# Modulation of a three-block model in unsplit float32 on four column groups, and HGRN states kept in place

## The chip, the cores and the metric

One core of a Trainium2 chip. The metric is the device time of one execution in microseconds (us). Kernel lines (L286) are those of the kernel before.

## The reference, cut to what matters

Two hybrid layers over 1024 latent and 256 context positions, width 1024, then a second block (state space model, latent attention, feed forward). All is float32. Each layer is modulated by vectors computed from a condition:

```
shift, scale, gate = split(c_act @ w_mod + b_mod, 3)          # latent: one row, 1024 x 3072, per layer
shift_c, scale_c, gate_c = split(cc_act @ w_mod + b_mod, 3)   # context: another row, same weights
lat = split_cols((rms_norm(h, norm_g) * (1 + scale) + shift) @ w_in)
...
s_new = exp(a_last) * state + einsum("bhsk,bhsv->bhkv", kc * exp(a_last - a), vc)   # HGRN, chunk by chunk
inter = einsum("bhtk,bhkv->bhtv", qc * exp(a), state)
...
h_new = h + gate * y
```

The second block has one more such modulation (1024 x 6144). Three products of two rows by a wide matrix are 24 row blocks of 512 columns.

## The kernel before, in words

Activations lie transposed, channels on partitions. Precision: a float32 operand is split into a high part (`wh`, cast on ACT to float32r) and a low part (`wl`, the remainder, subtracted on POOL or DVE), and a product is three matmuls of parts. `weights` (L194) makes them: 512 columns at a time it loads a raw tile (`wr`), casts `wh` (L203) and subtracts `wl` (L204). The pool `wp` holds 3 raw, 6 high and 6 low tiles, shared by all projections (`project`, L331: two tiles each, matmuls on L344, block by block) and by the modulation.

`modulation` (L275) makes one row block per step of a generator. For each of 4 pieces of 1024 columns it takes the split weights and multiplies both parts by the stationary condition (128 x 4: both rows, high and low): 16 matmuls (L286) into rows 0 to 3 of a PSUM tile. ACT copies the row (L288), four transposes (L291) turn it, and DVE adds bias and parts (L294, L296):

```
row = self.psum()[0:4]
parts = self.weights(w[j // 4, c], 1024, 512, subs, raws)
PE.matmul(row, act[:, 2 * c + k, :], parts[k][i], ...)
PE.transpose(t[:, 4 * i:4 * i + 4], r[:, i * P:(i + 1) * P], self.ident[0:4, 0:4])
```

The first four blocks run at the start (`inputs` in `first_block`, L1014), with a pool of 14 raw tiles and subtractions on DVE and POOL in turn. The other 20 are `self.filler`: `fill` (L173) takes one after every second projection of the two layers; their subtractions are on DVE.

The order of work: `hybrid_mix` (L972) runs a main chain, Fourier, attention (`gqa`), HGRN (`hgrn`), and beside it a lane of projections. At places of the main chain `dense(us)` takes as much of the lane as the budget says, by the numbers that the lane yields (a modulation block yields 24 x 0.213). The tile framework then schedules all instructions in that priority onto each engine's queue, with the buffers that each tag has, and writes the waits. Loads and stores are on SP's queue.

HGRN (L679) works on two channel halves c. Per direction it forms gates, sums them in chunks of 128 by a scan on DVE (L718), makes turned keys (tag `sc`), chunk sums `u` (L742), and then the states entering each chunk, `st` (L751), one step per chunk, of `st`, `ea` and `u`; a block's output (L833) takes them. The mask of its levels (L816) is uint32.

Of the kernel before, what the change touches and what calls it, by code (L numbers as in the profile page):

```python
# [14 lines left out]
U32 = mybir.dt.uint32  # L15
# [6 lines left out]
P = 128  # L22
# [58 lines left out]
GQA_STEPS = 4, 4, 0.5  # L81
MLA_STEPS = 3, 5, 0.4
# [7 lines left out]
class Kern:  # L90


    def __init__(self, tc, ctx):
        self.tc = tc
        self.nc = nc = tc.nc
        self.V, self.G, self.S, self.PE = nc.vector, nc.gpsimd, nc.scalar, nc.tensor
        self.const = ctx.enter_context(tc.tile_pool(name="const", bufs=1))
        self.tp = ctx.enter_context(tc.tile_pool(name="tp", bufs=2))
        self.dram = ctx.enter_context(tc.tile_pool(name="dr", bufs=1, space=DRAM))
        self.ps = ctx.enter_context(tc.tile_pool(name="ps", bufs=2, space=PSUM))  # L100
        self.flip = 0
        self.pending = None
        self.filler = iter(())
        self.calls = 0
        self.lane, self.owed = iter(()), 0.0
# [5 lines left out]
    def setup(self, io):  # L111
        V, G, S = self.V, self.G, self.S

        def const(name, shape, dt=F32):
            t = self.const.tile(list(shape), dt, name=name)
            self.load(t, io[name])
            return t

        self.vecs = const("vecs", (P, NVEC))
        self.ident = const("ident", (P, P))  # L120
        self.bd2 = const("bd2", (P, 2))
        self.one = self.const.tile([P, 1], F32, name="one")
# [3 lines left out]
        self.act = []  # L126
        for b in range(2):
            t = self.const.tile([P, 8, 4], F32R, name=f"act{b}")
            for s in range(2):
                a = act[:, 2 * b + s, :].rearrange("p (k o) -> p k o", o=1)  # L130
                S.activation(t[:, :, s:s + 1], a, AF.Copy)
                V.tensor_tensor(t[:, :, 2 + s:3 + s], a, f32(t)[:, :, s:s + 1], op=ALU.subtract)
            self.act.append(t)
# [60 lines left out]
    def weights(self, ap, n, width=P, subs=None, raws=None):  # L194

        out = []
        for a in range(0, n, WTILE):
            m = min(WTILE, n - a)
            raw = (raws or self.wp).tile([P, WTILE], F32, tag="wr", name="wr", bufs=14 if raws else 3)[:, :m]
            hi = self.wp.tile([P, WTILE], F32R, tag="wh", name="wh", bufs=6)[:, :m]  # L200
            lo = self.wp.tile([P, WTILE], F32R, tag="wl", name="wl", bufs=6)[:, :m]
            self.load(raw, ap[:, a:a + m])
            self.S.activation(hi, raw, AF.Copy)  # L203
            (next(subs) if subs else self.G).tensor_tensor(lo, raw, f32(hi), op=ALU.subtract)  # L204
            out += [(hi[:, k:k + width], lo[:, k:k + width]) for k in range(0, m, width)]
        return out
# [68 lines left out]
    def modulation(self, w, act, bias, tiles, out, subs=None, raws=None):  # L275


        V, PE = self.V, self.PE
        subs = subs or cycle((V,))
        for j in tiles:  # L280
# [6 lines left out]
            r = self.tmp("sp")[0:4]  # L287
            self.S.activation(r, row, AF.Copy)  # L288
# [3 lines left out]
            tv = t[:, :16].rearrange("p (i a) -> p i a", a=4)  # L292
            u = self.tmp("mu", (P, 4, 2))
            V.tensor_tensor(u, tv[:, :, 0:2],  # L294
                            bias[:, j:j + 4].rearrange("p (i o) -> p i o", o=1).to_broadcast([P, 4, 2]), op=ALU.add)
            V.tensor_tensor(out[:, j:j + 4], u, tv[:, :, 2:4], op=ALU.add)  # L296
            yield 24 * MM
# [170 lines left out]
    def weigh(self, pool, out, keys, n, scores, v, beside, pieces, steps):  # L468
# [5 lines left out]
        tail, ahead, wait = steps  # L474
# [6 lines left out]
        def count(i, e):  # L481
# [3 lines left out]
            elif len(sums[E]) == 1:  # L485
                total = self.ctmp(pool, "ea" if E is G else "eb", (P, 512), 2)[:, :n]
# [6 lines left out]
        for i, j in enumerate(keys):  # L493
            s = scores(j)
            e = self.ctmp(pool, "e", (P, 512), 13)[:, :n]
# [183 lines left out]
    def hgrn(self, pool, layer, src, need_ctx, y):  # L679
# [18 lines left out]
        mask = pool.tile([P, len(HG_LEVELS), P], U32, name="hg_mask")  # L698
        self.load(mask, self.io["hg_mask"])
        rst = pool.tile([P, 512], F32, name="rst")  # L700
        G.memset(rst, 1.0)
        G.memset(chunked(rst)[:, :, 0:1], 0.0)
        for c in range(2):
# [10 lines left out]
            for d, nm in ((0, "ff"), (1, "fb")):  # L714
                a, k = self.hgrn_gates(pool, src[f"{nm}{c}"], layer, d, c)
                for t0, n in ALL:
                    s = a[:, t0:t0 + n] if d == 0 else a[:, t0:t0 + n][:, ::-1]
                    V.tensor_tensor_scan(s, rst[:, :n], s, 0.0, op0=ALU.mult, op1=ALU.add)  # L718
# [12 lines left out]
                for t0, n in ALL:  # L731
                    kts.append(self.ctmp(pool, "sc", (P, 512), 3))
                    turned(kts[-1][:, :n], e, t0, n)
                for (t0, n), kt in zip(ALL, kts):
# [8 lines left out]
            state = []  # L743
            for d in range(2):
                st = pool.tile([P, nc_, 64], F32, tag=f"st{d}", name="st")
# [3 lines left out]
                G.memset(st[:, order[0]], 0.0)  # L749
# [3 lines left out]
                state.append(st)  # L753
# [5 lines left out]
    def hgrn_block(self, pool, layer, c, t0, n, src, vt, state, mask, cum, key, y):  # L759
# [10 lines left out]
        acc = [self.ctmp(pool, "sc", (P, 512), 3)[:, :n] for _ in range(2)]  # L770
# [56 lines left out]
        for j in range(m):  # L827
            cs = slice(j * P, (j + 1) * P)
            for h in range(2):
                r = slice(64 * h, 64 * h + 64)  # L830
                PE.matmul(o[r, cs], vt[:, j * P + 64 * h:j * P + 64 * h + 64], acc[h][:, cs], start=True, stop=False)
                for d in range(2):
                    PE.matmul(o[r, cs], state[d][r, c0 + j], qd[d][r, cs], start=False, stop=d == 1)  # L833
# [15 lines left out]
    def fourier(self, pool, src, t0, n, chan, alt, pos, y):  # L849
# [39 lines left out]
        for c in range(2):  # L889
# [24 lines left out]
            w = pool.tile([P, T], F32, tag="fy", name="fy", bufs=2)  # L914
            sn = pool.tile([P, T // 2], F32, tag="fs", name="fs", bufs=2)
# [8 lines left out]
    def hybrid_out(self, pool, layer, y, src, w_out, h_old, gate, t0, n, beside):  # L924
# [5 lines left out]
        for k in HYBRID_ORDER:  # L930
# [6 lines left out]
            a = pool.tile([P, 512], F32R, tag="yb", name="yh", bufs=20)[:, :n]  # L937
            b = pool.tile([P, 512], F32R, tag="yb", name="yl", bufs=20)[:, :n]
# [33 lines left out]
    def hybrid_mix(self, layer, io, x, need_ctx, inputs, close_x):  # L972
# [15 lines left out]
        with pool_of("fo") as fp:  # L988
# [4 lines left out]
            a = self.ctmp(fp, "fs", (P, T // 2), 2)  # L993
# [3 lines left out]
            a = self.ctmp(fp, "fs", (P, T // 2), 2)  # L997
# [16 lines left out]
    def first_block(self, io):  # L1014
# [12 lines left out]
        def inputs():  # L1027
            with tc.tile_pool(name="start", bufs=6, side="left", reuse_waits="tile") as sp:
                first = self.modulation(io["w_mod"][0], self.act[0], self.vec("b_mod", 0, 24), (8, 12, 0, 4), mod[0],
                                        cycle((V, self.G, V)), sp)  # L1030
# [26 lines left out]
            self.modulation(io["w_mod"][0], self.act[0], self.vec("b_mod", 0, 24), (16, 20), mod[0]),  # L1057
            self.modulation(io["w_mod"][1], self.act[0], self.vec("b_mod", 24, 24), range(0, 24, 4), mod[1]),
            self.modulation(io["w_mod_2"], self.act[1], self.vec("b_mod_2"), range(0, 48, 4), mod2))
# [20 lines left out]
        y, src = self.hybrid_mix(1, io, x, False, inputs1(y, src, xp, x), xctx.close)  # L1080
        self.rp = self.rows.enter_context(tc.tile_pool(name="rows", bufs=1, side="right", reuse_waits="tile"))
# [728 lines left out]
    def weight_pool(self, bufs):  # L1810
        ctx = ExitStack()
        self.wp = ctx.enter_context(self.tc.tile_pool(name="wp", bufs=bufs, side="left", reuse_waits="tile"))
        return ctx
# [79 lines left out]
    def run(self, io, out):  # L1893
        self.io = io
        self.setup(io)
        with ExitStack() as self.rows, self.weight_pool(3):
            self.second_block(io, *self.first_block(io), out)

# [22 lines left out]
def _constants():  # L1921
# [7 lines left out]
    m = np.zeros((P, len(HG_LEVELS), P), np.uint32)  # L1929
# [3 lines left out]
    c["hg_mask"] = m  # L1933
    k = np.arange(512)
# [118 lines left out]
```

## Time and profile before

| | |
|---|---|
| median of 3 runs | 4120.85 us (4118.63 to 4126.01) |
| profiled execution | 4121.71 us, span 4119.5 us |
| TensorE (PE) busy | 3827.2 us, 93% |
| weight loads (PEld) | 2892.6 us, 70% |
| DVE, ACT, POOL | 2426.4, 1683.2, 1536.1 us |
| mean granted clock of TensorE | 0.962 of full speed |
| HBM | 377.39 MB read, 119.21 MB written |

Busy times of matmuls are sums of single durations, which overlap in the pipeline; how long a run of matmuls takes is read from their starts. A float32 matmul is recorded as two instructions. Each group's idle time is that of its engine just before its instructions, with what ended it. The granted clock has two levels, 1.2 and 2.4 GHz; a mean of 0.95 over a stretch says that a tenth of it was at the lower one.

### The profile page before, as it was taken

How to read it: one execution, taken by the hardware profiler on the slowest of the kernel's cores; microseconds unless marked ns; L12 is line 12 of the kernel's file. 1: busy time of each engine (PE TensorE's matmuls, PEld its weight loads, DVE VectorE, ACT ScalarE, POOL GpSimd, SP SyncE). 2: the span in 40 equal slices, each digit the busy share in tenths (PEclk: the TensorE clock that was granted, in tenths of full speed). 3: DMA queues.
4: the chain of work that ended last, by engine and by line, in shares of the span. 5: the costliest groups of instructions: out<-in, count | busy, mean ns of one | idle time of the engine just before them, and what ended most of it. 6: DMA issues, size and time to landing. Idle time of an engine off the chain costs nothing.

```text
span 4119.5 us, 55376 instructions
## 1 busy us (share of the span) xinstructions
PE 3827.2 (93%) x19562; PEld 2892.6 (70%) x19562; DVE 2426.4 (59%) x4210; ACT 1683.2 (41%) x3047; POOL 1536.1 (37%) x1336
## 2 busy tenths in 40 slices
PE   6999999999999988988899988999999989999998
PEld 3765576667775567767667666665567979988986
DVE  7355587855446587768867776665565374324321
ACT  5333444345424445345434253444444343333332
POOL 3223301125314422146222133555555444445443
PEclk8999999999999989989999999999999989999999
DMA  5541222256552221164354567452223463343232
GB/s 180 170 130 61 65 75 93 83 165 212 174 161 64 70 74 58 63 206 146 118 161 147 183 184 209 116 147 63 50 51 110 136 208 102 93 117 121 93 114 83
DMA packets 273913, 500.25 MB, mean 121 GB/s; under 512 B 30978, under 2 KB 76578, under 8 KB 270628
## 3 DMA queue, kind: packets, MB, share of 16 engines
q1 hardware_dynamic: 269636, 467.75, 36.2%
q0 software_dynamic: 4000, 28.97, 3.0%
q8 instruction: 154, 2.52, 0.3%
q14 instruction: 123, 1.01, 0.1%
HBM read 377.39 MB, written 119.21 MB: 121 GB/s over the span
## 4 chain that ended last, share of the span: by engine, by line
PE 37%; DVE 11%; DMA 4%; ACT 2%; issue 2%; POOL 1%; SPq 0%; DVEq 0%; ACTq 0%; POOLq 0%
PE mm L213 22%; PE mm L344 5%; PE o L510 4%; DVE sm L459 3%; DVE sp L1161 2%; PE mm L1346 1%; DVE eb L487 1%; PE o L1563 1%; PE t L1585 1%; PE t L1357 1%; PE t L1358 1%; PE t L1520 1%; PE t L1356 1%; ACT sw L1553 1%; DMA xt<-xtok 0%
## 5 line engine op out<-in xcount | busy, mean ns | idle before, releaser
L204 POOL TENSOR_TENSOR wl<-wr,wh 128x512 fp32r<-128x512 f32 (+2 forms) x641 | 860.3, 1349 | 1568.0 <-ACT wh L203 1299.5
L203 ACT ACTIVATE wh<-wr 128x512 fp32r<-128x512 f32 (+1 forms) x822 | 503.2, 620 | 812.6 <-PE mm L213 250.7
L344 PE MATMUL mm<-xh,wh 128*128 128x512 f32 (+1 forms) x1704 | 664.1, 391 | 10.0 <-DVE sp L169 2.9
L344 PE MATMUL mm<-xh,wl 128*128 128x512 f32 (+1 forms) x1704 | 648.3, 381 | 6.6 <-POOL wl L204 6.5
L344 PE MATMUL mm<-xl,wh 128*128 128x512 f32 (+1 forms) x1704 | 648.9, 381 | 1.0 <-POOL xl L324 0.9
L496 ACT ACTIVATE e<-t 128x512 f32<-128x512 f32 (+1 forms) x488 | 284.0, 594 | 278.6 <-PE t L1358 125.7
L344 PEld LDWEIGHTS mm<-xh,wh 128*128 128x128 f32 x1704 | 329.9, 194 | 93.0 <-issue 19.7
L490 POOL TENSOR_TENSOR ea<-ea,e 128x512 f32<-128x512 f32 x240 | 325.5, 1356 | 170.1 <-ACT e L496 161.8
L344 PEld LDWEIGHTS mm<-xh,wl 128*128 128x128 f32 x1704 | 329.3, 193 | 75.0 <-POOL wl L204 10.6
L344 PEld LDWEIGHTS mm<-xl,wh 128*128 128x128 f32 x1704 | 330.2, 194 | 71.1 <-issue 13.5
L213 PE MATMUL mm<-fxh,wh 128*128 128x512 f32 (+2 forms) x1056 | 339.2, 322 | 2.9 <-ACT fxh L1737 2.1
L213 PE MATMUL mm<-fxh,wl 128*128 128x512 f32 (+2 forms) x1056 | 341.0, 323 | 0.0
L213 PE MATMUL mm<-fxl,wh 128*128 128x512 f32 (+2 forms) x1056 | 340.4, 322 | 0.3 <-DVE fxl L1738 0.2
L459 DVE TENSOR_REDUCE sm<-mm 128x1 f32<-128x512 f32 (+1 forms) x384 | 207.6, 589 | 17.3 <-PE mm L1346 16.7
L213 PEld LDWEIGHTS mm<-fxh,wh 128*128 128x128 f32 x1056 | 201.2, 191 | 19.2 <-ACT fxh L1737 2.6
L213 PEld LDWEIGHTS mm<-fxl,wh 128*128 128x128 f32 x1056 | 201.5, 191 | 17.4 <-DVE fxl L1738 1.6
L213 PEld LDWEIGHTS mm<-fxh,wl 128*128 128x128 f32 x1056 | 201.7, 191 | 15.6
L204 DVE TENSOR_TENSOR wl<-wr,wh 128x512 fp32r<-128x512 f32 x181 | 137.3, 771 | 68.8 <-ACT wh L203 66.1
L510 PE MATMUL o<-e,v 128*64 128x512 f32 x640 | 175.8, 602 | 0.0
L487 POOL TENSOR_TENSOR ea<-e 128x512 f32<-128x512 f32 (+1 forms) x52 | 65.8, 1265 | 237.0 <-ACT e L496 204.5
L1775 DVE TENSOR_SCALAR fc<-gs,vecs 128x512 f32<-128x512 f32 x44 | 54.1, 1231 | 165.8 <-ACT gs L1771 165.8
L459 DVE TENSOR_REDUCE sm<-t 128x1 f32<-128x512 f32 (+1 forms) x200 | 112.3, 589 | 55.3 <-PE t L596 53.8
(470 smaller groups left out, 8079.7 us busy)
## 6 DMA issues: line engine op xcount, KB each, us to landing
wr<-w_mod SPq DMA_DIRECT2D x192, 256.0 KB, 3.0
wr<-w_in SPq DMA_DIRECT2D x190, 256.0 KB, 2.9
wr<-w_up SPq DMA_DIRECT2D x176, 256.0 KB, 2.7
wr<-w_out SPq DMA_DIRECT2D x144, 256.0 KB, 3.1
wr<-w_down SPq DMA_DIRECT2D x80, 256.0 KB, 2.7
q<-qd POOLq DMA_DIRECT2D x16, 768.0 KB, 6.4
rope<-rope SPq DMA_DIRECT2D x20, 512.0 KB, 4.2
k<-kd POOLq DMA_DIRECT2D x16, 640.0 KB, 7.4
```

Of the source, the lines that this page charges most:

```text
L203: self.S.activation(hi, raw, AF.Copy)
L204: (next(subs) if subs else self.G).tensor_tensor(lo, raw, f32(hi), op=ALU.subtract)
L213: self.PE.matmul(out, a, b, start=i == 0, stop=i == n - 1)
L344: self.PE.matmul(ps, a, b, start=at + i == 0, stop=at == k_tiles - 1 and i == 2)
L459: V.tensor_reduce(m[:, a, c:c + 1], scores(a, c), axis=AX.X, op=ALU.max, negate=True)
L487: E.tensor_tensor(total, sums[E][0], e, op=ALU.add)
L490: E.tensor_tensor(sums[E][0], sums[E][0], e, op=ALU.add)
L496: S.activation(e, s, AF.Exp)
L510: PE.matmul(o[h:h + 64], v(j), e, start=i < 2, stop=i >= len(keys) - 2)
L1161: V.scalar_tensor_tensor(c, u[:, s0 + a:s0 + a + n], cw[:, a:a + 1], c, op0=ALU.mult, op1=ALU.add)
L1346: PE.matmul(s, qt[h][:, 0, t0 + a * P:t0 + (a + 1) * P], kt[h][:, 0, c0:c0 + w])
L1775: V.tensor_scalar(c, gs[:, o:o + 512], w[:, 0:1], b, op0=ALU.mult, op1=ALU.add)
```

## The change

1. Modulation. The weights are not split: a float32 tile of 512 columns (`mr`) is the moving operand. The stationary operand (`mact`) is 128 x 32 per piece, the two rows and 30 zero columns; piece k of 8 goes to column group k % 4 (rows 32(k % 4) onward of the PSUM tile), so each group gets two accumulating matmuls. ACT copies all 128 rows (`mrow`), and four matmuls with a constant 128 x 2 (`mod_sum`: ones at rows 0, 32, 64, 96 and 1, 33, ...) turn and sum them; this is done one block later. DVE adds the bias. The loads of a block are issued at the projection after the block before (`prefetch`); at the start 14 pieces are ahead. A block yields 16 x 0.213, and each of the three calls has one more step.
2. `wp` gets 4 high and 4 low tiles in the two layers, 6 and 6 in the second block (closed and opened again between, after the filler has run out), besides 8 `mr` tiles.
3. HGRN: states are written over the chunk sums `u`, the zero state is left out (8 clears, 8 matmuls less); the scan runs in pieces of 256; `sc` has 2 buffers instead of 3, the keys are turned one block ahead; the mask is uint8.
4. Buffers: attention's exponentials 13 to 10 in GQA, one `eb`; Fourier's `fy` and `fs` 2 to 1; output's split inputs 20 to 18.

```diff
-    def modulation(self, w, act, bias, tiles, out, subs=None, raws=None):
+    def modulation(self, w, block, bias, tiles, out, more=None):
...
-            row = self.psum()[0:4]
-            for c in range(4):
-                parts = self.weights(w[j // 4, c], 1024, 512, subs, raws)
-                for k in range(2):
-                    for i in range(2):
-                        PE.matmul(row, act[:, 2 * c + k, :], parts[k][i], start=c + k + i == 0, stop=c + k + i == 5)
...
-                PE.transpose(t[:, 4 * i:4 * i + 4], r[:, i * P:(i + 1) * P], self.ident[0:4, 0:4])
...
+        act = self.mod_act(block)
+        pieces = [(j, k) for j in tiles for k in range(8)]
+        ahead = 14 if more else 8
...
+        def turn(j, r):
+            t = self.psum()
+            for i in range(4):
+                PE.matmul(t[:, 2 * i:2 * i + 2], r[:, i * P:(i + 1) * P], self.mod_sum)
...
+        due.extend(range(ahead))
+        load()
+        self.prefetch = load
+        behind = None
+        for i, (j, k) in enumerate(pieces):
+            if k == 0:
+                load()
+                row = self.psum()
+            c = slice(32 * (k % 4), 32 * (k % 4) + 32)
+            PE.matmul(row[c], act[:, k], ws.pop(i), start=k < 4, stop=k >= 4)
+            due.append(i + ahead)
+            if more:
+                load()
+            if k == 7:
+                if behind:
+                    turn(*behind)
+                r = self.ctmp(self.wp, "mrow", (P, 512), 1)
+                self.S.activation(r, row, AF.Copy)
+                behind = j, r
+                yield 16 * MM
+        turn(*behind)
+        yield 1.0
...
         wks = [self.weights(w, k_tiles * P) for w in ws]
+        self.prefetch()
...
-            hi = self.wp.tile([P, WTILE], F32R, tag="wh", name="wh", bufs=6)[:, :m]
+            hi = self.wp.tile([P, WTILE], F32R, tag="wh", name="wh", bufs=self.wbufs)[:, :m]
...
-                for t0, n in ALL:
-                    s = a[:, t0:t0 + n] if d == 0 else a[:, t0:t0 + n][:, ::-1]
+                for t0 in range(0, TA, 256):
+                    s = a[:, t0:t0 + 256] if d == 0 else a[:, t0:t0 + 256][:, ::-1]
...
-                for a, b in zip(order, order[1:]):
-                    V.scalar_tensor_tensor(st[:, b], st[:, a], ea[:, d, a:a + 1], u[:, d, a],
-                                           op0=ALU.mult, op1=ALU.add)
+                for i, (a, b) in enumerate(zip(order, order[1:])):
+                    if i:
+                        V.scalar_tensor_tensor(u[:, d, a], state[d][a], ea[:, d, a:a + 1], u[:, d, a],
+                                               op0=ALU.mult, op1=ALU.add)
+                    state[d][b] = u[:, d, a]
```

Two places show how instructions move. DVE's order at the first HGRN gates of layer 0 (`wl` is a low part, `a0` the gates, the scan is the one on `rst`), before:

```order
L204 TENSOR_TENSOR wl_4333<-wr_4331,wh_4332 128x512
L666 SCALAR_TENSOR_TENSOR a0_4235<-gx_4233,gx_4234 128x1280
L204 TENSOR_TENSOR wl_4339<-wr_4337,wh_4338 128x512
L667 TENSOR_TENSOR k0_4236<-a0_4235,gx_4233 128x1280
L204 TENSOR_TENSOR wl_4349<-wr_4347,wh_4348 128x512
L718 SCALAR_TENSOR_TENSOR a0_4235<-rst_4193,a0_4235 128x512 x2
L718 SCALAR_TENSOR_TENSOR a0_4235<-rst_4193,a0_4235 128x256
L204 TENSOR_TENSOR wl_4355<-wr_4353,wh_4354 128x512
L722 TENSOR_TENSOR gx_4248<-a0_4235 128x1280
L294 TENSOR_TENSOR mu_4370<-mm_4365,vecs_66 128x8
```

and now:

```order
L697 SCALAR_TENSOR_TENSOR a0_3901<-gx_3899,gx_3900 128x1280
L698 TENSOR_TENSOR k0_3902<-a0_3901,gx_3899 128x1280
L749 SCALAR_TENSOR_TENSOR a0_3901<-rst_3849,a0_3901 128x256 x5
L753 TENSOR_TENSOR gx_3916<-a0_3901 128x1280
L163 COPY cux_4096<-mm_4165 128x256
L756 TENSOR_TENSOR gx_3916<-gx_3916,k0_3902 128x1280
L303 TENSOR_TENSOR mod1_88<-mm_4214,vecs_66 128x8
```

The low parts of a modulation block stood between the gates' steps, one behind the scan; now none does, and of the modulation DVE keeps the bias. SP's queue at the start (`h` are the tiles of x), before:

```order
L142 DMA bd_70<-bd 128x2
L142 DMA wr<-w_mod 128x512 x24
L142 DMA h_0_337<-xT 128x512
...
L142 DMA h_7_351<-xT 128x512
L142 DMA wr<-w_mod 128x512 x8
L142 DMA wr<-w_in 128x512 x3
```

and now:

```order
L136 DMA bd_70<-bd 128x2
L136 DMA mod_sum<-mod_sum 128x2
L136 DMA mr<-w_mod 128x512 x32
L136 DMA h_0_217<-xT 128x512
...
L136 DMA h_7_231<-xT 128x512
L136 DMA wr<-w_in 128x512 x3
```

The last eight pieces of the first four blocks stood behind x and stand ahead of it now.

## Rows read from the trace of the kernel before

**Rows 1.** The page, part 1: busy us, share of the span, instructions.
```profile
PE 3827.2 (93%) x19562; PEld 2892.6 (70%) x19562; DVE 2426.4 (59%) x4210; ACT 1683.2 (41%) x3047; POOL 1536.1 (37%) x1336
```
**Rows 2.** Stretches: us; busy us of PE, PEld, DVE, ACT, POOL; PEclk; DMA.
```profile
60.00:500.00 440.00, 410.89 (x1863) 273.79 (x1861) 224.87 (x427) 169.27 (x297) 136.78 (x131) 0.94 0.32 102
500.00:910.00 410.00, 378.47 (x2305) 283.50 (x2306) 315.71 (x698) 172.06 (x291) 52.73 (x43) 0.96 0.31 100
...
1060.00:1460.00 400.00, 377.26 (x1674) 247.43 (x1673) 208.96 (x360) 165.23 (x269) 131.27 (x113) 0.95 0.37 116
1460.00:1760.00 300.00, 270.04 (x1555) 209.15 (x1554) 221.85 (x437) 125.03 (x178) 57.20 (x47) 0.96 0.21 67
```
**Rows 3.** Groups by line, PE, 60 to 1500 us: busy us, mean ns, idle before.
```profile
L344 PE MATMUL mm<-xh,wl 128*128 128x512 f32 (+1 forms) x977 | 363.6, 373 | 1.8 <-POOL wl L204 1.7
...
L286 PE MATMUL mm<-wl,act 128*4 128x512 f32 x160 | 66.8, 418 | 28.8 <-DVE wl L204 28.6
L286 PE MATMUL mm<-wh,act 128*4 128x512 f32 x160 | 65.8, 411 | 8.8 <-ACT wh L203 8.7
...
L291 PE MATMUL mm<-ident,sp 4*128 4x4 f32 x80 | 9.5, 221 | 7.2 <-ACT sp L288 7.1
```
**Rows 4.** Timeline, PE, one modulation block in HGRN: start, us, instruction, idle before.
```profile
503.77 0.40 PE L286 MATMUL mm<-wl,act 128*4 128x512 f32 x1 [1.22 <-DVE wl L204]
504.00 0.39 PE L286 MATMUL mm<-wh,act 128*4 128x512 f32 x1
...
510.20 0.59 PE L286 MATMUL mm<-wl,act 128*4 128x512 f32 x1 [3.42 <-DVE wl L204]
```
**Rows 5.** Timeline, DVE, the same block.
```profile
503.03 0.69 DVE L204 TENSOR_TENSOR wl<-wr,wh 128x512 fp32r<-128x512 f32 x1
...
505.63 3.93 DVE L718 TENSOR_TENSOR_SCAN a<-rst,a 128x512 f32<-128x512 f32 x3
```
**Rows 6.** Timeline, PE, attention of the second block: float32 matmuls in two column groups.
```profile
2559.43 1.93 PE L510 MATMUL o<-e,v 128*64 128x512 f32 x6
2561.29 0.38 PE L1346 MATMUL mm<-k,q 128*128 128x256 f32 x1
2561.61 1.08 PE L510 MATMUL o<-e,v 128*64 128x512 f32 x4
2562.61 0.51 PE L1346 MATMUL mm<-k,q 128*128 128x512 f32 x1
```
**Rows 7.** Timeline, PE: the transposes of a first block; small float32 matmuls.
```profile
14.83 0.41 PE L291 MATMUL mm<-ident,sp 4*128 4x4 f32 x4 [0.68 <-ACT sp L288]
15.17 0.40 PE L286 MATMUL mm<-wh,act 128*4 128x512 f32 x1
...
181.70 1.84 PE L249 MATMUL t<-bd,sq 128*128 128x2 f32 x16
```
**Rows 8.** 13 half-clock stretches, columns as in rows 2: last, sum; L286 alone.
```profile
1446.50:1460.20 13.70, 7.51 (x25) 3.78 (x26) 11.78 (x15) 7.99 (x13) 2.54 (x2) 0.50 0.44 139
sum 95.60, PE 76.45 PEld 52.16 DVE 64.42 ACT 43.05 POOL 39.57; mean PE 5.88 PEld 4.01 DVE 4.96 ACT 3.31 POOL 3.04
...
sum 95.60, PE 15.09 PEld 2.13; mean PE 1.16 PEld 0.16
```
**Rows 9.** Timeline, PE, the start: sums of squares and first projections.
```profile
35.42 1.86 PE L249 MATMUL t<-one,acc 128*128 128x1 f32 x8 [5.04 <-DVE acc L314]
...
48.34 0.50 PE L344 MATMUL mm<-xh,wh 128*128 128x512 f32 x1
...
87.28 0.61 PE L249 MATMUL t<-one,acc 128*128 128x1 f32 x4
...
91.43 1.22 PE L344 MATMUL mm<-xh,wh 128*128 128x256 f32 x3 [1.18 <-ACT xh L326]
```
**Rows 10.** Groups by line, ACT and POOL, 60 to 1500 us.
```profile
L203 ACT ACTIVATE wh<-wr 128x512 fp32r<-128x512 f32 x296 | 182.2, 626 | 244.8 <-PE mm L344 105.9 <-DMA wr<-w_mod 42.6 <-DMA wr<-w_in 35.8
...
L204 POOL TENSOR_TENSOR wl<-wr,wh 128x512 fp32r<-128x512 f32 x136 | 193.6, 1436 | 586.6 <-ACT wh L203 417.6 <-DVE sc L814 54.8 <-DVE hw L795 40.5
```

More of the change, by code (lines that the diff above doesn't have):

```diff
@@ L1 @@
 from contextlib import ExitStack
-from itertools import chain, cycle
+from itertools import chain
 import numpy as np
@@ L125, in setup @@
         S.activation(act.rearrange("p a k -> p (a k)"), self.vec("act"), AF.Silu)
[L126 to L133, printed above, removed]
+        self.act = act
+        self.mod_sum = const("mod_sum", (P, 2))
         self.qg = self.const.tile([P, 2], F32, name="qg")
@@ L192, in dense_to, with weights @@
             self.owed = 0.0
-    def weights(self, ap, n, width=P, subs=None, raws=None):
+    def weights(self, ap, n, width=P):
         out = []
@@ L271, in split, with mod_act @@
         self.V.tensor_tensor(lo, x, f32(hi), op=ALU.subtract)
-    def modulation(self, w, act, bias, tiles, out, subs=None, raws=None):
-        V, PE = self.V, self.PE
-        subs = subs or cycle((V,))
-        for j in tiles:
-            row = self.psum()[0:4]
-            for c in range(4):
-                parts = self.weights(w[j // 4, c], 1024, 512, subs, raws)
-                for k in range(2):
-                    for i in range(2):
-                        PE.matmul(row, act[:, 2 * c + k, :], parts[k][i], start=c + k + i == 0, stop=c + k + i == 5)
-            r = self.tmp("sp")[0:4]
-            self.S.activation(r, row, AF.Copy)
+    def mod_act(self, block):
+        t = self.ctmp(self.wp, "mact", (P, 8, 32), 1)
+        self.G.memset(t, 0.0)
+        for s in range(2):
+            self.V.tensor_copy(t[:, :, s:s + 1], self.act[:, 2 * block + s, :].rearrange("p (k o) -> p k o", o=1))
+        return t
@@ new lines, in modulation, with load @@
+    def modulation(self, w, block, bias, tiles, out, more=None):
+        V, PE = self.V, self.PE
+        act = self.mod_act(block)
+        pieces = [(j, k) for j in tiles for k in range(8)]
+        ahead = 14 if more else 8
+        ws, due = {}, []
+        def load():
+            for i in due:
+                if i < len(pieces):
+                    j, k = pieces[i]
+                    if i % ahead < 8:
+                        ws[i] = self.wp.tile([P, 512], F32, tag="mr", name="mr", bufs=8)
+                    else:
+                        ws[i] = more.tile([P, 512], F32, tag="mr", name="mr", bufs=6)
+                    self.load(ws[i], w[j // 4, k // 2][:, 512 * (k % 2):512 * (k % 2) + 512])
+            due.clear()
+        def turn(j, r):
@@ L473, in weigh @@
         V, G, S, PE = self.V, self.G, self.S, self.PE
-        tail, ahead, wait = steps
+        tail, ahead, wait, ebufs = steps
         o = self.psum("o")[:, :n]
@@ L730, in hgrn, with keys_turned @@
                 kts = []
[L731 to L734, printed above, removed]
+                def keys_turned(b):
+                    if b < len(ALL):
+                        t0, n = ALL[b]
+                        kts.append(self.ctmp(pool, "sc", (P, 512), 2))
+                        turned(kts[-1][:, :n], e, t0, n)
+                keys_turned(0)
+                for b, (t0, n) in enumerate(ALL):
+                    keys_turned(b + 1)
+                    kt = kts[b]
                     self.dense(HGRN_WAIT[1])
@@ L769, in hgrn_block @@
         self.silu2(q, q, temp())
-        acc = [self.ctmp(pool, "sc", (P, 512), 3)[:, :n] for _ in range(2)]
+        acc = [self.ctmp(pool, "sc", (P, 512), 2)[:, :n] for _ in range(2)]
         def halves(t, b):
@@ L831, in hgrn_block @@
                 PE.matmul(o[r, cs], vt[:, j * P + 64 * h:j * P + 64 * h + 64], acc[h][:, cs], start=True, stop=False)
-                for d in range(2):
-                    PE.matmul(o[r, cs], state[d][r, c0 + j], qd[d][r, cs], start=False, stop=d == 1)
+                ds = [d for d in range(2) if c0 + j in state[d]]
+                for d in ds:
+                    PE.matmul(o[r, cs], state[d][c0 + j][r], qd[d][r, cs], start=False, stop=d == ds[-1])
         os_ = temp()
@@ L1895, in run @@
         self.setup(io)
-        with ExitStack() as self.rows, self.weight_pool(3):
+        with ExitStack() as self.rows:
+            self.weight_pool(4)
             self.second_block(io, *self.first_block(io), out)
+            self.wctx.close()
 def _cols(*vs):
@@ L1933, in _constants @@
     c["hg_mask"] = m
+    c["mod_sum"] = np.stack([i % 32 == 0, i % 32 == 1], axis=1).astype(np.float32)
     k = np.arange(512)
```

67 lines of the change are left out of this document (31 added, 36 removed).

## The prediction

> **What bounds the kernel now.** I read the page first. TensorE is busy 93% of the span and the next engine, DVE, 59% [rows 1]: the kernel is a chain of matmuls, and time comes off it by removing matmul work, by removing waits ahead of matmuls, or by a higher granted clock. Then I read the span by stage, over the two layers that the change touches [rows 2]: projections, Fourier and attention (60 to 500 us), HGRN of layer 0 (500 to 910), the same two of layer 1 (1060 to 1460 and 1460 to 1760). TensorE is busy 90 to 94% in each, at a mean granted clock of 0.94 to 0.96. Only in the HGRN stages does a second engine come near: DVE 315.7 of 410 us. Next come the groups of TensorE's instructions with their idle time [rows 3]. The modulation's three lines (L286 twice, L291) hold 28.8 + 8.8 + 7.2 = 44.8 us of idle time between 60 and 1500 us, nearly all ended by the low part of its weights, its high part and the copy of its row. The projections beside them (L344) wait 1.8 us for a low part. So the modulation's blocks are where TensorE stands still.
>
> One such block, in the timeline, shows why [rows 4]. Its matmuls follow each other in 0.23 us while the weights are there (503.77 to 504.00); the one at 510.20 comes after 3.42 us of idle, for a low part. DVE spent that time on the HGRN scan, 3.93 us [rows 5]; the subtraction stood behind it in DVE's order. After such a stop the clock is at half.
>
> **What the change takes away and adds.** After the first four blocks, which run at the start, 20 blocks of the modulation lie among other work.
>
> Gone per block: 16 matmuls and 4 transposes. At the warm pace that is 320 x 0.23 = 73.6 us and 20 x 0.34 = 6.8 us (14.83 to 15.17 is four transposes) [rows 4, 7]. With the idle time: 73.6 + 6.8 + 44.8 = 125.2 us. The idle time goes because the new matmuls read the loaded float32 tile itself, issued one block ahead: no cast and no subtraction stands before them, and the row is turned a block later.
>
> Added per block: 8 float32 matmuls over four column groups, and 4 small float32 matmuls. The trace has float32 matmuls on two column groups, in attention (L510), each recorded as two instructions [rows 6]. A pair, one on each group, takes 2562.61 - 2561.61 = 1.00 us to the next instruction. Three take 2561.29 - 2559.43 = 1.86 us, so one alone adds 0.86. The second group is thus nearly free; nothing shows four. Bounds for a block of eight: 2 x 1.00 = 2.0 us if four overlap as two do, 4 x 1.00 = 4.0 if only two overlap, 8 x 0.86 = 6.9 if none. I take 2.0, since the recorded pair is the nearest row and nothing in it looks used up. Going back to full width costs 0.2 us: the 256-column L1346 holds the engine 0.32 us before the next pair. The small matmuls: 8 recorded instructions at 1.84 / 16 = 0.115 us, 0.92 us [rows 7]. Per block 2.0 + 0.2 + 0.9 = 3.1, in all 62 us. Net: 125 - 62 = **63 us less**.
>
> Here the Trainium skill speaks too. "TensorE: Matmul & The Clock Gate", Part 3, gives 2.38 times for three column groups; by the same share four would take some 1.1 us a round, an estimate from that page, and the sum would be 4 us higher. I stay with the row.
>
> **Clock.** 13 stretches at half clock begin in or just after one of the 20 blocks: 95.6 us, in which TensorE is busy 76.5 us, 15.1 of them the modulation's matmuls [rows 8]. The other 61 us would take half at full clock: 0 to 30 us to gain. The HGRN stage without blocks (1460 to 1760) also runs at 0.96, so other waits bring the clock down as well and some stretches will come back. I take **20 us less**.
>
> **Start.** The first projection matmul comes at 48.34, 12.9 us after the sums of squares reach TensorE at 35.42 [rows 9]. The same chain for the context block, where DVE has nothing else, takes 91.43 - 87.28 = 4.15 us at the end of the same window. At half clock and 512 columns I allow 6. The subtractions that stood between its steps are gone, and all four blocks run before x lands; but x is now loaded behind 32 pieces instead of 24, eight transfers of 256 KB. **8 us less** (bounds 3 and 11).
>
> **What may cost.** The split weights of all projections now have 4 + 4 buffers instead of 6 + 6. A projection needs two tiles of each, so one set is in use and one is being made. A cast is 0.63 us, a subtraction on POOL 1.44 [rows 10], against at least 2.8 us that a set is in use (24 matmuls, at half of 0.23 for 256 columns); TensorE hides it. Uncovered it would cost the rival below. The scan in 5 pieces of 256 instead of 3: its 3.93 us stay, by columns, or become 6.6, by pieces; times 8 scans that is 0 to 21 us on DVE, and in HGRN DVE has lost 8 blocks x 8 subtractions x 0.69 = 44 us [rows 5]; I take 2. The Fourier and output buffers (2 to 1, 20 to 18) each delay a few preparations by about one 1.3 us step: 3. Each of the three calls of the modulation issues its first eight loads only when it begins, and has one more step that only turns a row: 5. The exponentials' 10 buffers equal the keys of a pass, whose sums are drained before the next pass reaches the same buffer; HGRN's states save 8 small matmuls and its clears: 0. Together **10 us more** (0 to 30).
>
> **Sum.** The profiled execution took 4121.7 us, 0.9 above the median of the runs: 4121.7 - 63 - 20 - 8 + 10 = 4040.7, and 4040 against the median.
>
> **Rivals.**
> *Only two groups overlap at once.* Then a block takes 4.0 us and the sum is 40 higher: **4080**. For it: the trace shows no more than two. Against it: a pair ends 0.14 us after one alone would, so groups cost each other little.
> *HGRN's chain takes the gain back.* In 500 to 910 DVE, not TensorE, may set the pace; the eight blocks there then give nothing for their 8/20 of 63 us: **4066**. Against it: DVE loses 44 us there too.
> *No overlap.* An unsplit float32 matmul costs 0.86 us where two split ones cost 0.46. Eight serial ones are 6.9 us: 20 x 4.9 = 98 higher, **4138**, slower. The pair in rows 6 speaks against it. The Trainium skill, "FP8 and Floating Point Precision", TensorE Precision Notes, counts four passes for true float32; by that rule alone this rival would be the likeliest, and only the groups' overlap in the row keeps it small.
> *The short ring of weights.* Its place is every projection and output matmul of the two layers, 94 calls (27 + 27 of the lane, 40 of the output). If ACT reaches the casts late because a cast waits for TensorE to free a buffer with other work queued behind it, TensorE then stands 0.63 + 1.44 = 2.1 us a call: 195 us in all, **4235**; from 39 calls on it eats the whole gain. For it: ACT already stands 105.9 us before casts until TensorE frees a buffer [rows 10]. Against it: that wait says the ring is filled early, and L344 hardly waits.
>
> **Chances.** Forecast 0.60; two groups 0.13; HGRN 0.09; no overlap 0.06; short ring 0.12. About 0.2% (8 us) is what a measurement of this kernel can tell from no change. Faster: 0.60 + 0.13 + 0.09 and the ring where it decides in few calls, 0.02: 0.84. Same: 0.04, the ring near break-even. Slower: 0.12. The range takes in the forecast's bounds. Low: all of the clock's 30, the start's 11, nothing lost, and some of the half-clock time of the stages that rows 2 show beyond those 13 stretches (the three with blocks lose 63 us to the clock, another 25 of it): 4121 - 63 - 30 - 11 - 25 = 3990; I go to 3980. High: two groups, no clock gained: 4100.
>
> **What would show it.** Right: the new matmul's line starts four instructions together and a block is past in about 3 us; no idle time ahead of it; the subtraction on DVE gone; granted clock of 60 to 500 above 0.95; first projection matmul near 40 us. Wrong: idle time ahead of L344's successor ended by POOL or ACT casts (the ring); pairs instead of fours; HGRN of layer 0 still 410 us long. Much below 3980 would mean that more waits hung on the modulation's casts than stand before its own matmuls.

## The result, and the profile after

The changed kernel takes **4069.85 us** (median of 4 runs, 4061.25 to 4073.72) against 4122.72 (4118.63 to 4126.01) before: a ratio of **0.9869, 95% interval 0.985 to 0.9889**. Faster as forecast, inside the range, but with 53 us won, not the 81 of the forecast's 4040. In the profiled executions 4073.72 stands against 4121.71, 48.0 us less. Lines below are those of the changed kernel, or where a run's own line differs, of that run.

The page, part 1, after (busy us, share, instructions), beside [rows 1]:

```profile
PE 3803.0 (93%) x19642; PEld 2889.4 (71%) x19642; DVE 2291.3 (56%) x4017; ACT 1575.1 (39%) x2851; POOL 1515.7 (37%) x1321
```

DVE lost 135 us and ACT 108, TensorE 24: the split is gone, and TensorE is as full as before. Groups of TensorE, 60 to 1500 us, after (busy, mean ns, idle before), beside [rows 3]:

```profile
L375 PE MATMUL mm<-yh,wl 128*128 128x512 f32 (+1 forms) x192 | 72.1, 377 | 5.0 <-POOL wl L198 5.0
...
L375 PE MATMUL mm<-yh,wh 128*128 128x512 f32 (+1 forms) x192 | 70.9, 379 | 14.2 <-ACT yh L978 13.8 <-ACT wh L197 0.3
...
L315 PE MATMUL mm<-mr,mact 128*32 128x512 f32 x320 | 49.6, 661 | 1.0 <-DVE sp L443 1.0
...
L302 PE MATMUL mm<-mod_sum,mrow 128*128 128x2 f32 x152 | 19.8, 252 | 0.0
```

Of the kernel before, the line that the second of these stands against:

```profile
L344 PE MATMUL mm<-yh,wh 128*128 128x512 f32 (+1 forms) x192 | 70.2, 367 | 4.5 <-ACT yh L939 4.3 <-ACT xh L326 0.2
```

The modulation's lines (L315, L302) wait 1.0 us where they waited 44.8. What grew is the wait ahead of the first part of the output projection's operands, from 4.5 to 14.2 us, 9.0 of them at one matmul. (The busy time of a group counts overlapped time once: the 320 durations of L315, 0.661 us in the mean and 211 us in sum, lie in 49.6 us.) One block in the timeline, beside [rows 4]:

```profile
165.65 1.92 PE L315 MATMUL mm<-mr,mact 128*32 128x512 f32 x16
167.50 1.05 PE L302 MATMUL mm<-mod_sum,mrow 128*128 128x2 f32 x8
168.41 0.48 PE L375 MATMUL mm<-xh,wh 128*128 128x512 f32 x1
```

Eight float32 matmuls (16 recorded) take 1.92 us, and the block is past in 168.41 - 165.65 = 2.76. Of the 20 blocks behind the start, 14 go at this pace; the other six have matmuls of other work among theirs or run in part at half clock. The start, beside [rows 9]:

```profile
36.08 1.87 PE L243 MATMUL t<-one,acc 128*128 128x1 f32 x8 [5.63 <-DVE acc L344]
41.87 1.12 PE L260 MATMUL t<-ident,rsy 128*128 128x128 f32 x4 [3.92 <-DVE rsy L230]
44.58 1.22 PE L375 MATMUL mm<-xh,wh 128*128 128x512 f32 x2 [1.60 <-ACT xh L356]
```

Stretches after (us; busy of PE, PEld, DVE, ACT, POOL; granted clock; DMA), beside [rows 2] but shifted to the same work: before the HGRN mixer, and both stages of layer 1.

```profile
60.00:500.00 440.00, 423.23 (x2070) 293.14 (x2071) 205.12 (x395) 160.51 (x272) 148.12 (x138) 0.98 0.35 113
...
1010.00:1410.00 400.00, 384.80 (x1793) 258.17 (x1792) 176.29 (x312) 141.91 (x232) 137.99 (x119) 0.98 0.38 121
1410.00:1705.00 295.00, 264.54 (x1530) 201.02 (x1529) 213.58 (x442) 119.65 (x168) 37.47 (x34) 0.94 0.19 62
```

The clock rose to 0.98 where attention runs and did not in the HGRN stage (0.94, was 0.96). Over the span it is 0.965 against 0.962.

**Where the time is lost again.** Two stages: HGRN of layer 0, from its first matmul to the first output matmul, and the output projection of layer 0, from there to its last. Before:

```profile
491.98:908.91 416.93, 384.94 (x2351) 288.18 (x2350) 317.79 (x701) 176.59 (x295) 51.65 (x43) 0.96 0.32 101
908.91:1038.91 130.00, 121.93 (x602) 102.17 (x600) 72.83 (x109) 69.19 (x125) 81.25 (x61) 0.95 0.68 213
```

After:

```profile
469.24:853.09 383.85, 356.00 (x2225) 275.21 (x2225) 268.32 (x629) 133.94 (x220) 46.24 (x35) 0.95 0.28 91
853.09:999.42 146.33, 130.57 (x599) 105.47 (x600) 90.43 (x121) 73.21 (x135) 86.11 (x63) 0.92 0.64 204
```

At the first output matmul (908.91, now 853.09) the changed kernel is 55.8 us ahead; the output projection, in which no modulation runs, gives 16.3 back. All stages of the two traces, after less before: start -3.8 us, from there to HGRN -19.0, HGRN of layer 0 -33.1, its output projection +16.3, layer 1 up to HGRN -11.8, HGRN of layer 1, with three blocks in it instead of one, +1.1, the rest +2.7, together some -47.5. What opens the output projection, on ACT: the first gate `z` (tile `nt`) that it prepares. Before, then after:

```profile
882.88 0.64 ACT L935 ACTIVATE nt<-nt 128x512 f32<-128x512 f32 x1 [6.91 <-DMA nt<-cz]
```

```profile
846.29 0.63 ACT L974 ACTIVATE nt<-nt 128x512 f32<-128x512 f32 x1
```

And on TensorE, the first output matmul, before and after:

```profile
908.91 0.39 PE L344 MATMUL mm<-yh,wh 128*128 128x512 f32 x1
```

```profile
853.09 0.80 PE L375 MATMUL mm<-yh,wh 128*128 128x512 f32 x1 [8.98 <-ACT yh L978]
```

Before, ACT began 26.0 us ahead of TensorE, because 125 matmuls of the lane still stood between the last HGRN matmul (sums of squares, L249, now L243) and the first output matmul. After, 26 stand there; ACT begins 6.8 us ahead, TensorE stands 9.0 us and goes on at half clock (granted clock 0.50 up to 858.00, 0.80 us an instruction).

### The profile page after: what moved, and what is told of

Read it like the earlier page. It is cut to its first block, busy times and chain, and to the rows that moved or that the text cites. A ratio compares the mean times of both kernels' runs of the same rounds, so it can differ in the third digit from the quotient of the medians.

```text
span 4072.0 us, 54955 instructions
## 1 busy us (share of the span) xinstructions
PE 3803.0 (93%) x19642; PEld 2889.4 (71%) x19642; DVE 2291.3 (56%) x4017; ACT 1575.1 (39%) x2851; POOL 1515.7 (37%) x1321
## 4 chain that ended last, share of the span: by engine, by line
PE 39%; DVE 11%; DMA 3%; ACT 2%; issue 2%; POOL 1%; SPq 0%; DVEq 0%; ACTq 0%; POOLq 0%
PE mm L207 23%; PE mm L375 4%; PE o L541 4%; DVE sm L490 3%; DVE sp L1202 2%; PE mm L1387 1%; PE t L1626 1%; PE o L1604 1%; DVE eb L518 1%; PE t L1561 1%; PE t L1398 1%; PE t L1399 1%; DMA xt<-xtok 1%; PE t L1397 1%; DVE sp L1199 1%
## 5 line engine op out<-in xcount | busy, mean ns | idle before, releaser
L198 POOL TENSOR_TENSOR wl<-wr,wh 128x512 fp32r<-128x512 f32 (+1 forms) x630 | 842.7, 1343 | 1653.2 <-ACT wh L197 1587.6
L375 PE MATMUL mm<-xh,wh 128*128 128x512 f32 (+1 forms) x1704 | 657.2, 386 | 11.8 <-ACT xh L356 4.4
L197 ACT ACTIVATE wh<-wr 128x512 fp32r<-128x512 f32 (+1 forms) x630 | 386.7, 619 | 697.6 <-PE mm L207 261.0
L375 PE MATMUL mm<-yh,wh 128*128 128x512 f32 (+1 forms) x320 | 123.8, 396 | 24.9 <-ACT yh L978 18.6
L207 PE MATMUL mm<-fhh,wh 128*128 128x512 f32 x352 | 137.0, 389 | 0.0
```

The lines of the kernel that those rows point to most:

```text
L198: self.G.tensor_tensor(lo, raw, f32(hi), op=ALU.subtract)
L207: self.PE.matmul(out, a, b, start=i == 0, stop=i == n - 1)
L375: self.PE.matmul(ps, a, b, start=at + i == 0, stop=at == k_tiles - 1 and i == 2)
```

## Experiments

Stages are cut as above, each from the one profiled execution of its run; "cover" counts the lane's matmuls that start after the end of the last HGRN matmul (L249, L243) and before the first output matmul of layer 0. Ratios are to the kernel before, run on the same chip in the same batch.

| run | ratio (95%) | HGRN 0, us (clock) | output 0, us | cover |
|---|---|---|---|---|
| before | 1 | 416.9 (0.96) | 130.0 | 125 |
| after | 0.9869 (0.985 to 0.9889) | 383.9 (0.95) | 146.3 | 26 |
| lane24 | 0.9853 (0.9837 to 0.9869) | 372.6 (0.97) | 145.3 | 77 |
| lane32 | 0.9895 (0.9876 to 0.9914) | 386.2 (0.94) | 143.7 | 158 |
| lane40 | 0.9949 (0.993 to 0.9968) | 396.0 (0.91) | 140.7 | 206 |
| lane24yb20 | 0.987 (0.9846 to 0.9895) | 377.4 (0.95) | 144.2 | 77 |
| lane24yb20sc | 0.9843 (0.9826 to 0.986) | 370.1 (0.98) | 146.1 | 77 |
| lane28yb20sc | 0.9848 (0.9835 to 0.9862) | 374.6 (0.95) | 140.8 | 116 |
| lane32yb20sc | 0.987 (0.9851 to 0.9888) | 386.3 (0.93) | 134.7 | 158 |
| oldmod6 | 1.0035 (1.0023 to 1.0047) | 417.5 (0.96) | 137.5 | 125 |
| oldmod6yb20 | 1.003 (1.0019 to 1.0041) | 422.1 (0.95) | 128.5 | 125 |
| oldmod4yb20 | 1.011 (1.0094 to 1.0126) | 441.7 (0.93) | 131.5 | 125 |
| groups1 | 1.0059 (1.0047 to 1.0071) | 406.7 (0.98) | 145.1 | 26 |
| groups2 | 0.9918 (0.9903 to 0.9934) | 383.9 (0.97) | 145.7 | 26 |

### Do the four column groups overlap?

**groups1**: all on one group.

```diff
-            c = slice(32 * (k % 4), 32 * (k % 4) + 32)
-            PE.matmul(row[c], act[:, k], ws.pop(i), start=k < 4, stop=k >= 4)
+            c = slice(0, 32)
+            PE.matmul(row[c], act[:, k], ws.pop(i), start=k == 0, stop=k == 7)
```

> The changed kernel with all eight matmuls of a modulation block on the first column group, one behind the other (the small turning matmul then sums 32 rows). If the four groups overlap as the trace suggests (1.9 us for eight) and the gain of the change hangs on that: eight take 8 x 0.86 = 6.9 us, 5.0 us more for each of the 20 blocks behind the start and somewhat more at the start, so 4165 to 4185 us, slower than the kernel before by 1.0 to 1.5%. If the gain came from the split that was taken off ACT and DVE and from the idle ahead of the blocks, and PE has slack: under 4120 us.

**groups2**: `32 * (k % 2)`, `start=k < 2, stop=k >= 6`.

> The changed kernel with the matmuls of a modulation block on two column groups in turn, four on each. One group made 4140.5 us against 4115 before, that is 3.9 us for each of 20 blocks over the changed kernel. If the groups run beside each other in full, four rounds of one matmul's time: about 3.5 to 3.8 us for eight against 1.9 with four groups, 4090 to 4100 us. If only neighbours in a pair can overlap, and four groups are no better than two: the same as the changed kernel, 4060 us on this chip.

The same block of layer 0 in the timeline, on one group:

```profile
177.82 7.05 PE L315 MATMUL mm<-mr,mact 128*32 128x512 f32 x16
184.80 1.05 PE L302 MATMUL mm<-mod_sum,mrow 32*128 32x2 f32 x8
185.78 0.50 PE L375 MATMUL mm<-xh,wh 128*128 128x512 f32 x1
```

and on two:

```profile
166.72 3.63 PE L315 MATMUL mm<-mr,mact 128*32 128x512 f32 x16
170.28 1.05 PE L302 MATMUL mm<-mod_sum,mrow 64*128 64x2 f32 x8
171.26 0.50 PE L375 MATMUL mm<-xh,wh 128*128 128x512 f32 x1
```

7.05, 3.63 and 1.92 us on one, two and four groups: 8, 4 and 2 rounds of 0.88 to 0.96 us each. The groups run almost fully beside each other. On one group the change would be a loss (4140.53 us, 1.0059), about what the no-overlap rival gave, 4138. Both runs are below what was expected of them (4083.62 us for two groups), since the whole moved less than the blocks: 20 x (7.96 - 2.76) = 104 us longer on TensorE, but 0.0190 x 4115 = 78 us measured, and 20 x (4.54 - 2.76) = 36 against 0.0049 x 4115 = 20 (each good to some 10 us by the intervals). With the longer blocks the mean granted clock is 0.968 to 0.970 in all executions of both, against 0.963 to 0.967 in those of the changed kernel: a denser TensorE seems to give part of it back.

### Did the lane run dry, and is that the loss?

**lane24**, **lane32**, **lane40**: how many matmuls' worth a block tells `dense` that it was.

```diff
-                yield 16 * MM
+                yield 24 * MM
```

> The changed kernel with the lane's account of a modulation block set back from 16 to 24 matmuls, so that fewer lane matmuls are drawn for each block. Theory A (the lane of projections runs dry before the HGRN mixer of layer 0 ends, which leaves the 9.0 us gap ahead of the first output matmul and an output projection that opens without cover): the lane has some 90 matmuls (20 us) left at the end of the mixer as the kernel before had, the gap of 9 us goes, the output projection of layer 0 falls from 146 us towards 135, and the time is 4055 to 4063 us. Theory B (shorter rings of split weights and of output operands cost those 16 us): the gap may close but the output projection stays at 143 to 148 us, and the time is 4063 to 4072 us. Theory C (the gap only moves: what the lane no longer does early it must do later, at PE's own cost): no change, 4067 to 4073 us.

> The changed kernel with a modulation block counted as 32 matmuls. Between the last HGRN matmul and the first output matmul of layer 0 stood 125 lane matmuls in the kernel before, 26 in the changed one and 77 with 24. Theory A (those lane matmuls are the cover under which ACT, DVE and SP prepare the first output operands; the output projection of layer 0 grew by 14 us only because that cover went): some 120 to 130 lane matmuls stand there, the output projection comes back to 128 to 136 us, and the time falls by 8 to 16 us under that with 24, to 4036 to 4046 us on a chip where the kernel before takes 4115. Theory B (the cover serves only the gap ahead of the first output matmul; the rest is another cost of the new modulation): the output projection stays at 143 us or more and the time at 4049 to 4058 us. Theory C (what is kept for the end is missing as cover between the HGRN matmuls): the output projection shortens but the HGRN stage grows by as much in idle.

> As the run before it, with 40 matmuls for a block: some 170 lane matmuls left for the end of layer 0. Theory A: the first output operands are ready before the lane ends, so no further gain; within 5 us of 32. Theory C: slower than 32 by 5 us or more, with more idle ahead of the HGRN matmuls.

lane24, first output matmul; then its HGRN and output stages, and HGRN of layer 1:

```profile
841.05 0.73 PE L375 MATMUL mm<-yh,wh 128*128 128x512 f32 x2 [0.99 <-ACT yh L978]
```

```profile
468.42:841.05 372.63, 348.86 (x2225) 271.03 (x2225) 269.15 (x629) 132.69 (x218) 47.26 (x34) 0.97 0.28 93
841.05:986.30 145.25, 129.73 (x599) 104.86 (x600) 90.20 (x121) 73.72 (x137) 89.33 (x65) 0.93 0.66 208
1357.71:1679.41 321.70, 287.33 (x1679) 220.74 (x1677) 232.11 (x464) 142.42 (x196) 42.29 (x37) 0.96 0.22 72
```

lane40, the same three:

```profile
468.31:864.31 396.00, 367.20 (x2226) 284.95 (x2227) 268.44 (x635) 136.65 (x223) 43.36 (x35) 0.91 0.28 93
864.31:1005.04 140.73, 126.73 (x601) 104.46 (x600) 83.08 (x115) 70.37 (x131) 86.40 (x63) 0.94 0.63 198
1374.02:1727.79 353.77, 314.69 (x1678) 239.87 (x1677) 233.97 (x463) 142.51 (x197) 44.51 (x37) 0.87 0.20 66
```

At 24 (4052.28 us) the gap closes (8.98 to 0.99 us) and the HGRN stage shortens by 11.2 us, as theory A said; the output projection stays at 145, which is theory B. With more cover it shortens by a few us only, and the kernel gets slower (4073.47 us, then 4095.65). Theory C is right in its effect and wrong in its mechanism: the HGRN stage of layer 0 grows from 372.6 to 396.0 us with the same matmuls (2225 and 2226 recorded), but of these 23.4 us only some 5 are idle time; 18.3 are a longer busy time (348.9 to 367.2). Its clock falls from 0.97 to 0.91, and in layer 1 from 0.96 to 0.87. That isn't one trace alone: over all their executions the mean granted clock is 0.966 to 0.970 in lane24, 0.961 to 0.964 in lane32, 0.954 to 0.959 in lane40. One half-clock stretch of lane40's HGRN stage, in two parts, and what followed it:

```profile
541.40:555.10 13.70, 12.61 (x50) 7.36 (x47) 5.07 (x10) 0.00 (x0) 0.00 (x0) 0.50 0.04 11
555.10:561.90 6.80, 6.80 (x33) 6.47 (x32) 2.55 (x4) 1.67 (x3) 1.35 (x3) 0.50 0.10 39
561.90:565.30 3.40, 2.67 (x22) 1.03 (x22) 2.89 (x11) 1.54 (x3) 0.71 (x1) 1.00 0.39 110
```

TensorE had stood 2.67 us before it, for DVE. In the first part it is busy for 12.6 of 13.7 us, with HGRN's own matmuls of 128 columns only, and the clock stays at half; 22 of the second part's 33 are the lane's, of 256 columns, and behind them the clock is full again. Another stretch, 592.6 to 619.9 us, goes the same way; in the HGRN stage of lane24 the longest is 13.7 us. So the lane's wider matmuls among HGRN's small ones kept the clock up or brought it back, and taken out to serve as cover later they leave it at half. This is read from where the stretches begin and end; which property of these matmuls does it was not tried. The cover costs where it came from.

### What do the smaller buffers and the other parts cost?

**oldmod6**, **oldmod6yb20**, **oldmod4yb20**: the old modulation put back in the changed kernel, with `self.weight_pool(6)` or `(4)`, and 18 or 20 `yb` buffers.

> Everything of the change but the modulation: the old modulation with split weights and six buffers of them, with HGRN states in place, the scan in five pieces, the one-byte mask, one buffer for the Fourier tables, 18 output operands. Theory A (these parts are about free): within 0.2% of the kernel before, 4114 to 4131 us. Theory B (the smaller buffers are the missing 36 us): 4140 to 4160 us, with the output projection of layer 0 at 140 us or more against 130 before. Theory C (states in place shorten the HGRN mixer's DVE chain): 4095 to 4112 us, with the mixer of layer 0 under 405 us against 417.

> As the run before it, with 20 buffers for the output operands in place of 18. Theory B (the ring of output operands sets the output projection of layer 0): at least 8 us faster than with 18 and the output projection back at 130 us. Theory A (the ring is long enough either way): the two within 5 us of each other.

> The old modulation with all other parts of the change and 20 output operands, but with four buffers of split weights in place of six. In the output projection no modulation runs, so its length prices the shorter ring by itself. Theory A (four buffers are too few there: the ACT cast of the last weights waits for PE and the operands of the next block wait behind it on ACT): the output projection of layer 0 goes from 128.5 us with six buffers to 135 to 140 us. Theory B (the ring is long enough; the growth to 145 us comes from the new modulation): it stays at 127 to 131 us. The whole should be slower than with six either way, since the old modulation uses the same ring: 4135 to 4200 us.

The output stage of layer 0 with 18, then with 20 operands:

```profile
906.44:1043.94 137.50, 125.58 (x601) 105.36 (x600) 85.67 (x115) 68.50 (x128) 83.41 (x61) 0.93 0.64 203
```

```profile
915.65:1044.14 128.49, 120.09 (x601) 101.03 (x600) 72.59 (x109) 69.57 (x126) 82.19 (x61) 0.96 0.69 216
```

18 operands cost this stage 9.0 us, as theory B had it; four buffers of split weights in place of six cost it 3.0 (131.5), little more than its theory B, while the whole is slower by 0.8% of the time (1.011 against 1.003): the old modulation draws on the same ring, as expected. Yet the two runs with six differ by 5.6 us at the end (4131.83 and 4126.19), with overlapping intervals: what 20 operands won was hardly seen there. Without the new modulation the other parts make the kernel 0.35% slower, 14 us (0.30%, 12 us, with 20 operands): none of the three theories' numbers, between A and B. With 20 operands it is not in the output stage. The traces show it in HGRN of layer 1 alone, 335.2 and 334.9 us against 327.8, at a clock of 0.93 against 0.95; HGRN of layer 0 took 417.5 and 422.1 against 416.9, so 5 us lie between two kernels that differ by two operand buffers alone up to there. It isn't traced to a line. The scan is not it, as far as DVE's time goes. In the HGRN stage of layer 0, before, and then with pieces of 256 (oldmod6yb20):

```profile
L718 DVE TENSOR_TENSOR_SCAN a<-rst,a 128x512 f32<-128x512 f32 x8 | 9.3, 1209 | 0.0
...
L718 DVE TENSOR_TENSOR_SCAN a<-rst,a 128x256 f32<-128x256 f32 x4 | 3.7, 922 | 0.0
```

```profile
L718 DVE TENSOR_TENSOR_SCAN a<-rst,a 128x256 f32<-128x256 f32 x20 | 13.1, 719 | 0.0
```

13.0 against 13.1 us. (In layer 1: 12.4 + 3.7 against 17.2. The 4.8 us in the expectation of lane24yb20sc left out the four short pieces of the kernel before.)

### Together

**lane24yb20**, **lane24yb20sc**, **lane32yb20sc**, **lane28yb20sc**: 24, 32 or 28 matmuls for a block, 20 operands, and for "sc" the scan in pieces of 512.

```diff
-            a = pool.tile([P, 512], F32R, tag="yb", name="yh", bufs=18)[:, :n]
+            a = pool.tile([P, 512], F32R, tag="yb", name="yh", bufs=20)[:, :n]
...
-                r = self.ctmp(self.wp, "mrow", (P, 512), 1)
+                r = self.tmp("sp")
```

> The kernel with the lane's account at 24 and with 20 output operands again; the place for them is made by keeping the copied row of the modulation in an existing ring and one small table of the second block out of the first. Theory A (output operands and split weights share the 15 us that the output projection of layer 0 lost, about half each): that stage goes from 145 to 135 to 139 us and the time is 5 to 12 us below the run with 18, at 4040 to 4048 us on a chip where the kernel before takes 4115. Theory B (the ring of split weights alone sets it): 143 us or more and no change of the time.

> As the run before it, and the scan of the HGRN gates in pieces of 512 columns again in place of 256. Theory A (the shorter pieces cost DVE time in front of the turned gates that PE waits for: 4.8 us of DVE in the mixer of layer 1 by the run with the old modulation): 4 to 9 us faster than the run before it, and the idle ahead of the turning matmuls smaller. Theory B (the cost of the states in place lies in the state matmuls, not in the scan): within 3 us.

> 32 matmuls for a block, 20 output operands and the scan in pieces of 512 columns. If the scan's 4.8 us of DVE in each layer and the output operands count once the lane covers the opening of the output projection: 5 to 12 us below the run with 32 alone. If not: within 4 us of it.

> Between the two: 28 matmuls for a block, 20 output operands, the scan in pieces of 512 columns. With 24 the HGRN stage of layer 0 took 370.1 us and the output projection 146.1, with 32 they took 386.3 and 134.7: the same cover, early or late. If the trade is even all along, 4048 to 4062 us and the two stages together 514 to 523 us. If some 110 lane matmuls at the end are enough to open the output projection and few enough to keep the clock up in the HGRN stage: 135 to 139 us and below 375 us, 4036 to 4046 us, the best of all.

The copied row now lies in the ring `sp`, so these runs differ by that too. lane32yb20sc, 4064.48, is 9 us below lane32, as its first branch had it, though the intervals touch; lane24yb20, 4062.07, stays above what was expected. Twenty operands alone help the output stage only when the cover is there: 144.2 for 145.3 us with 77 lane matmuls, 134.7 for 143.7 with 158. With 77 the operands are late whatever room there is; with 158 and 18 the room is missing. The stage needs both, and the cover that it needs costs the HGRN stage its clock: at 28 the two stages take 515.4 us, at 24 with "sc" 516.3, at 32 521.0. The trade is even between 24 and 28, as the first branch of the last expectation had it. The scan's pieces stay unsettled: the medians of the runs without and with it differ by 11 us, but their intervals overlap (the run without it spread from 4052.97 to 4082.11).

lane24, lane24yb20sc and lane28yb20sc have the lowest ratios, 0.9843 to 0.9853. Their intervals overlap that of the changed kernel, so that they beat it by some 0.2% is likely but not shown; all beat the kernel before. HGRN states in their own tiles again, with all else as changed, were not tried.

## Why the prediction was right, and what it mis-sized

- **What bounds the kernel**: right. TensorE stays at 93% with 24 us less work, and the block's removed waits went as such.
- **The 20 blocks, forecast 63 us less**: right and a little low. A block is 2.76 us where 3.1 was forecast, 1.0 us of idle is left: 125.2 - 20 x 2.76 - 1.0 = 69 us, at full clock. Taking a pair's overlap for four was right: 0.96 us a round where 1.00 was taken. The Trainium skill, "TensorE: Matmul & The Clock Gate", Part 3, lists 2.38 times for three column groups; here four gave 7.05 / 1.92 = 3.7 times, so the estimate of 1.1 us a round was too high. The four passes of true float32 that the Trainium skill, "FP8 and Floating Point Precision", TensorE Precision Notes, counts agree with the trace: 0.88 us for one of eight in a row against 0.23 for a split matmul.
- **The clock, forecast 20 us less (0 to 30)**: about 14 by the profiled executions: (1 - 0.962) x 4119.5 = 157 us lost to it before, (1 - 0.965) x 4072.0 = 143 after. Attention gained and HGRN did not. "Some stretches will come back" is what happened, and lane40 shows how.
- **The start, forecast 8 us less**: 48.34 to 44.58, 3.8 less, within its bounds of 3 and 11. The sums reach TensorE no earlier (36.08 against 35.42); the root's chain is what shortened, 8.5 us from there to the first projection matmul, where 6 was allowed.
- **What may cost, forecast 10 us (0 to 30)**: this is the term that was mis-sized. 69 + 14 + 4 = 87 us were won and 48.0 arrived, so it was some 39, beyond its own bound; that the time still lies in the range is owed to the range's width. Two parts of it stand in the changed kernel's trace: the gap ahead of the first output matmul, 9.0 us, gone in lane24, and the 16.3 us of the output projection of layer 0. Beside the old modulation, with 125 matmuls of cover, two fewer operands cost that stage 9.0 us and two fewer weight buffers 3.0; in lane24yb20, with 77, two more operands gave back only 1.1, so these prices hold only where the cover is there. A third part, some 14 us, is left for the other stages. The other parts of the change cost 12 us beside the old modulation (8 to 17 by the interval); that it is these 12 is likely but not shown. The prediction priced the buffers one by one as delays of a step of about 1.3 us, a step that stands in none of its rows. Its words "a block yields 16 x 0.213" stood in the change, and the sum never used them: that number is the budget by which the lane is drawn, and lowering it alone drew 51 of the 99 missing lane matmuls out of the end of layer 0 (77 stand there in lane24, 26 in the changed kernel). Layer 0 now also has 11 blocks instead of 13; that this is the rest was not tried.
- **Rivals**: two groups at once and no overlap are out (groups2, groups1). HGRN's chain took back a part. The stage of layer 0 went from 416.9 to 383.9 us, but 94 of its lane matmuls (1111 before, 1017 after; 239.6 and 220.9 us busy) now stand ahead of it, and TensorE waits longer for DVE ahead of the transposes of the gates, before and after:

```profile
L693 PE MATMUL t<-ident,gx 128*128 128x128 f32 x60 | 8.9, 298 | 2.6 <-DVE gx L725 2.6
```

```profile
L724 PE MATMUL t<-ident,gx 128*128 128x128 f32 x60 | 11.1, 335 | 11.0 <-DVE gx L756 9.5 <-DVE mod L303 1.0 <-DMA gx<-hi 0.5
```

  The measured time lies near this rival's 4066, but not for its reason: of some 18 us of idle time ahead of the eight blocks' lines there 1.0 is left, and 25 of the 39 us above stand at the output projection. The short ring of weights is real and small: 3.0 us in 40 output calls, and hardly a wait at the projections; what ACT shows is again that it fills the ring early, beside [rows 10]:

```profile
L197 ACT ACTIVATE wh<-wr 128x512 fp32r<-128x512 f32 x140 | 86.8, 625 | 159.7 <-PE mm L375 106.3 <-issue 28.2 <-DMA mr<-w_mod 7.7
```

## What to carry to other kernels

When a filler gets shorter, look for who counts by its length: the account that paces a lane is part of the change, and the work that it moves was covering something at both ends. Buffers that are priced one at a time hide each other; price the stage that needs several at once, with its cover gone. Wide matmuls among small ones paid twice here, since the clock stayed up where they stood, so taking them away can cost more than the time they took.

## What the runs showed that was not expected

Four column groups with float32 operands of 512 columns run with almost no loss: 7.05, 3.63 and 1.92 us for the same eight matmuls on one, two and four groups. And the same matmuls of the HGRN stage took 372.6 to 396.0 us by nothing but where the lane's matmuls stood, at a granted clock of 0.97 to 0.91: with 1.1 us of idle time among them, HGRN's small ones went on for 13.7 us at half clock.
